# A two-layer hybrid decoder trunk on one core: the first projection chunk taken from raw token blocks, layer 0's norm applied afterwards

## The chip, the core and the metric

The kernel runs on one core of one Trainium2 chip. The core has a matrix engine (TensorE, in the profile PE for its matmuls and PEld for its weight loads), a vector engine (VectorE, DVE), a scalar engine (ScalarE, ACT), a general engine (GpSimd, POOL) and a queue engine (SyncE, SP) that issues nearly all DMAs here. SBUF is the working memory with 128 partitions; PSUM takes the matmul results, in banks of 128 x 512 float32. The engines run their own instruction streams in order and wait for each other by semaphores. The metric is the device time of one launch in microseconds (us); lower is better.

## The reference

The input `x` is 512 tokens of 2048 features, all in float32. Two layers follow, each as `x = x + rms_norm(mixer(rms_norm(x, norm_pre)), norm_post)`.

```python
def rms_norm(x, w):
    y = x * rsqrt(mean(x * x, axis=-1) + EPS)
    return y * w
# layer 0 (even): z = h @ w_in, 2048 -> 7 * 1024, split into qa, fa, ia, ga, ub, vb, gb
#   8 recurrence heads from qa, fa, ia (chunked gated linear recurrence, then rms_norm) * silu(ga)
#   8 gating groups: layer_norm(vb) per 128 columns, causal 128 x 128 mixing, + bias, * ub * silu(gb)
#   concatenation @ w_out
# layer 1 (odd): multi-head latent attention with rotary keys, silu gate, @ w_out
```

What matters for the change: `h` is `x` scaled per token by one factor r (the reciprocal root mean square) and per feature by `norm_pre`. Every column of `z` is linear in `h`, so r can be applied to `z` instead of to `x`. For `vb`, which goes through a layer norm, r cancels but for the epsilon.

## The kernel before

**Precision.** Matmuls use operands that are rounded to the faster `float32r` form. To keep float32 accuracy each operand is split into a rounded part (`hi`, written by ScalarE as a cast) and the rest (`lo`, written by VectorE as a subtraction), and three matmuls take the place of one: hi x hi, hi x lo, lo x hi. `R` holds the split activations, transposed: `R[:, 2k]` and `R[:, 2k+1]` are hi and lo of features 128k to 128k+127 for all 512 tokens.

**Weights.** `plan_chunk` lists the weight pieces, each of 128 x 1024 elements (512 KB), in the order of use. `fetch(n)` issues the DMA of a piece into one of three `raw` buffers, `wload` splits it into `whi` and `wlo` (four buffers each), and `piece(n)` sees that pieces up to n + 3 are split. `proj_tok` computes a chunk with tokens on the partitions of the result (the activations are the stationary operand); `proj_feat` computes one with features on the partitions. `tick()` is called after each piece and runs the small tasks that `at(delay, ...)` has put off, so that the recurrence work lies between the matmuls.

**Order.** The code is traced as a list, and a planner then makes one fixed instruction stream for each engine out of it. It works by dependencies and its own cost estimates, with trace order as the priority, so an instruction whose inputs and buffers are free may be placed well ahead of its place in the code.

**The start.** The norm weights of layer 0 come by DMA into four partitions of `B`, and VectorE spreads them over all (line 352). For each of the four token tiles, `pre_norm` squares the four 512-feature blocks on ScalarE (line 290), sums them, makes r on GpSimd (lines 275, 276), multiplies x by r and the weights on VectorE (line 296), transposes on TensorE, four 128 x 128 transposes to a PSUM bank `tp` of which there are two (line 301), and splits the result into `R` (lines 283, 284). The first chunk, `ia` for two heads, is 256 columns wide; its first four pieces are taken token tile by token tile (`by="first"`), so that it can start when the first tile is normalized. The `ia` columns of all eight heads come as 256 (heads 0 and 1), 512 (heads 2 to 5) and 256 (heads 6 and 7).

**The later chunks of layer 0.** For each of four pairs of heads p, `fa`, `qa` and `ga` follow; their evacuations (`fa_evac` and so on) write PSUM to `W`, which held x until then. `hgrn_vec`, `hgrn_scores`, `hgrn_state`, `hgrn_out` and `hgrn_fin` are the recurrence. Then come two `gmlp` halves, the output projection, and layer 1. These take PSUM from four `mm` banks in turn.

Of the kernel before, what the change touches and what calls it, by code (L numbers as in the profile page):

```python
# [10 lines left out]
F32 = mybir.dt.float32  # L11
# [7 lines left out]
P = 128  # L19
T = 512  # L20
NT = T // P
# [23 lines left out]
def trunk_kernel(ctx, tc, x, positions, norm_pre, norm_post, ev_w_in, ev_lb_logits, ev_a_onorm,  # L45
# [9 lines left out]
    ptp = ctx.enter_context(tc.tile_pool(name="ptp", bufs=2, space=bass.MemoryType.PSUM))  # L55

    def mm_bank():
        return pmm.tile([P, 512], F32, name="mm", tag="mm")
# [30 lines left out]

    def row_bc(dst, src_row):  # L90
        nc.sync.dma_start(out=dst, in_=src_row.partition_broadcast(P))


    W = new_w("Wa")
    for c in range(4):
        (nc.vector if c % 2 else nc.gpsimd).memset(B[:, 4 + c, :], 0.0)
    nc.sync.dma_start(out=B[0:P:32, 4:8, :],
                      in_=norm_pre[0].partition_broadcast(4).rearrange("q (c n) -> q c n", c=4))
    for c in range(4):
        nc.sync.dma_start(out=W[:, c, :], in_=x_t[0][:, c * 512:(c + 1) * 512])  # L100

# [4 lines left out]

    pk = const.tile([18, P], F32, name="pk")
    nc.sync.dma_start(out=pk[0:16, :], in_=ev_lb_logits.rearrange("l (h p) -> (l h) p", p=P))
    nc.sync.dma_start(out=pk[16:17, :], in_=ev_a_onorm)
    nc.sync.dma_start(out=pk[17:18, :], in_=inv_freq)  # L110

# [20 lines left out]
    def wview(w):  # L132
        return w.rearrange("(k p) c -> p k c", p=P)
# [13 lines left out]
    def fetch(n):  # L147
        src, nk, nco, _ = plan[n]
        raw = ring.tile([P, 1024], F32, name="raw", tag="raw", bufs=3)
        nc.sync.dma_start(out=raw[:, 0:nk * nco].rearrange("p (k c) -> p k c", k=nk), in_=src)  # L150
        fetched[n] = raw

    def wload(i):
# [12 lines left out]
        lo = ring.tile([P, 1024], F32R, name="wlo", tag="wlo")  # L166
        if cuts is None:
            nc.scalar.copy(hi[:, 0:n], raw[:, 0:n])  # L168
            nc.vector.tensor_tensor(lo[:, 0:n], raw[:, 0:n], hi[:, 0:n].bitcast(F32), ALU.subtract)  # L169
# [25 lines left out]
    def at(delay, fn):  # L195
        seq[0] += 1
        tasks.append((clock[0] + delay, seq[0], fn))
# [117 lines left out]


    ew, ow = wview(ev_w_in[0]), wview(od_w_in[0])
    qv, kvv = wview(od_w_qb[0]), wview(od_w_kvb[0])
    cuts_q = ((0, 128), (128, 192))
    pl = {}  # L320
    for p in range(4):
        if p == 1:
            pl["ia", p] = plan_chunk(ew, IA + 256, 512, KD, 2)
        elif p != 2:
            pl["ia", p] = plan_chunk(ew, IA + 256 * p, 256, KD, 4)
        for nm_, c0 in (("fa", FA), ("qa", QA), ("ga", GA)):
            pl[nm_, p] = plan_chunk(ew, c0 + 256 * p, 256, KD, 4)
# [21 lines left out]

    wpre = [B[:, 4 + c, :] for c in range(4)]  # L350
    for c in range(4):
        nc.vector.stream_shuffle(wpre[c], wpre[c], [0] * 32)
    for i in range(NT):
        if i > 0:
            for c in range(4):
                nc.sync.dma_start(out=W[:, 4 * i + c, :], in_=x_t[i][:, c * 512:(c + 1) * 512])
            if i == 1:
                issue_to(3)
        else:
            for q in range(2):  # L360
                fetch(q)
        pre_norm(i, [W[:, 4 * i + c, :] for c in range(4)], wpre,
                 [B[:, 8 + 4 * (i % 2) + c, :] for c in range(4)], G[:, 8, :])

# [4 lines left out]
    def setup_masks():  # L369
# [14 lines left out]
        nc.vector.memset(pw, 1.0)  # L384
        nc.gpsimd.memset(G[:, 8, :], 0.0)

    setup_masks()
    S_sb = new_hs("S_sb", F32)
    nc.gpsimd.memset(S_sb, 0.0)

# [3 lines left out]
    def setup_rope():  # L394
        pi = G[:, 6, :].bitcast(I32)
        row_bc(pi, positions[0])
        ang, n, r = sinT, cosT, G[:, 6, :]
# [154 lines left out]
    for p in range(4):  # L552
        def ia_evac(i, ps, p=p):
            psv = ps.rearrange("p (h v) -> p h v", v=P)
            for a in range(0, psv.shape[1], 2):
                vp = 2 * ((p + a // 2) % 2)
                nc.scalar.copy(G[:, vp:vp + 2, i * P:(i + 1) * P], psv[:, a:a + 2])
# [8 lines left out]
        def ga_evac(m, ps):  # L566
            nc.scalar.activation(W[:, 6 + m, :], ps, AF.Sigmoid)
            nc.vector.tensor_tensor(W[:, 6 + m, :], ps, W[:, 6 + m, :], ALU.mult)
# [12 lines left out]

    def gmlp(s_):
# [4 lines left out]
        wsT = G[:, 0, :]  # L587
        row_bc(lnw[0], ev_b_ln_w[0, s_ * 512:(s_ + 1) * 512])
        row_bc(lnw[1], ev_b_ln_b[0, s_ * 512:(s_ + 1) * 512])
        row_bc(bias, ev_b_bias[0, 4 * s_:4 * s_ + 4].rearrange("g t -> (g t)"))  # L590
        nc.sync.dma_start(out=ws, in_=ev_b_ws[0, 4 * s_:4 * s_ + 4].rearrange("g t s -> t g s"))
        nc.gpsimd.affine_select(ws, ws, pattern=[[0, 4], [-1, P]], compare_op=ALU.is_ge, fill=0.0,
# [13 lines left out]
        def vb_evac(i, ps):  # L606
            for g in range(4):
                nc.vector.bn_stats(stats[:, i, g], ps[:, g * P:(g + 1) * P])
                nc.vector.bn_aggr(mv[:, i, g], stats[:, i, g])
            nc.gpsimd.tensor_scalar(rs[:, i], mv[:, i, :, 1], 1.0, EPS, ALU.mult, ALU.add)  # L610
            nc.gpsimd.tensor_tensor(rs[:, i], rs[:, i], mhalf[:, 0:4], ALU.pow)
# [24 lines left out]
        for e in range(2):  # L636
# [3 lines left out]
            def ub_evac(m, ps, U=U):  # L640
                nc.scalar.copy(U[:, m], ps)

            def gb_evac(m, ps, p=p, Z=Z, V=V):
                nc.scalar.activation(Z[:, m], ps, AF.Sigmoid)
                nc.vector.tensor_tensor(Z[:, m], ps, Z[:, m], ALU.mult)
                nc.vector.tensor_tensor(B[:, 8 + 2 * p + m, :], V[:, m], Z[:, m], ALU.mult)
# [359 lines left out]
```

## Time and profile before

| | |
|---|---|
| time, median of three runs | 1597.62 us (1597.39 to 1598.52) |
| time of the profiled execution | 1596.93 us |
| its span | 1595.2 us |
| TensorE busy, share of the span | 1568.3 us, 98% |
| VectorE busy | 750.8 us, 47% |
| ScalarE busy | 532.0 us, 33% |
| GpSimd busy | 95.7 us, 6% |
| DMA, mean over the span | 101 GB/s |

A row of the timeline gives the start from the beginning of the span, the duration, the engine, the line of the kernel, the operation, its output and inputs, a count where equal instructions are merged, and in brackets the idle time before it with what ended it. A row of the groups gives the count after the shapes, then the busy time in us and the mean duration of one in ns. A row of the stretches gives for each engine the busy time and, after x, the count of its instructions. A row of the waits gives the total, the number of waits and the longest. Matmuls overlap in the trace: the duration of one is longer than the distance to the next, and the distance is what a stream of them costs.

### The profile page before, as it was taken

How to read it: one execution, taken by the hardware profiler on the slowest of the kernel's cores; microseconds unless marked ns; L12 is line 12 of the kernel's file. 1: busy time of each engine (PE TensorE's matmuls, PEld its weight loads, DVE VectorE, ACT ScalarE, POOL GpSimd, SP SyncE). 2: the span in 40 equal slices, each digit the busy share in tenths (PEclk: the TensorE clock that was granted, in tenths of full speed). 3: DMA queues.
4: the chain of work that ended last, by engine and by line, in shares of the span. 5: the costliest groups of instructions: out<-in, count | busy, mean ns of one | idle time of the engine just before them, and what ended most of it. 6: DMA issues, size and time to landing. Idle time of an engine off the chain costs nothing. (4 is left out here: it accounts for less than half of the span.)

```text
span 1595.2 us, 19593 instructions
## 1 busy us (share of the span) xinstructions
PE 1568.3 (98%) x7841; PEld 1327.2 (83%) x7841; DVE 750.8 (47%) x1333; ACT 532.0 (33%) x904; POOL 95.7 (6%) x145
## 2 busy tenths in 40 slices
PE   6999999999999999999999999999999999999997
PEld 6888888898888888888887788888889988988886
DVE  7653455535434224353225743232266767762234
ACT  6422322222222222232224533222265555542221
POOL 1000000000014004000001000000000000000000
PEclk9999999999999999999999999999999999999999
DMA  7332222223234333243335523333221221332324
GB/s 221 118 92 80 92 93 80 80 80 99 91 102 119 99 98 101 94 151 100 102 103 172 150 78 102 93 93 98 87 75 55 70 60 52 102 106 94 105 93 158
DMA packets 118150, 160.95 MB, mean 101 GB/s; under 512 B 7830, under 2 KB 74408, under 8 KB 118056
## 3 DMA queue, kind: packets, MB, share of 16 engines
q1 hardware_dynamic: 118060, 159.71, 32.4%
q8 instruction: 61, 1.00, 0.3%
q14 instruction: 29, 0.24, 0.0%
HBM read 151.30 MB, written 8.39 MB: 100 GB/s over the span
## 5 line engine op out<-in xcount | busy, mean ns | idle before, releaser
L169 DVE TENSOR_TENSOR wlo<-raw,whi 128x1024 fp32r<-128x1024 f32 x240 | 296.8, 1238 | 641.3 <-ACT whi L168 624.8
L168 ACT CAST whi<-raw 128x1024 fp32r<-128x1024 f32 x240 | 252.3, 1052 | 779.1 <-PE mm L211 346.3
L209 PE MATMUL mm<-whi,R 128*128 128x512 f32 (+1 forms) x960 | 364.0, 379 | 0.5 <-ACT R L283 0.5
L210 PE MATMUL mm<-wlo,R 128*128 128x512 f32 (+1 forms) x960 | 362.1, 377 | 1.2 <-DVE wlo L169 1.2
L211 PE MATMUL mm<-whi,R 128*128 128x512 f32 (+1 forms) x960 | 362.1, 377 | 0.0
L214 PE MATMUL mm<-R,whi 128*128 128x512 f32 x832 | 326.1, 392 | 0.0
L216 PE MATMUL mm<-R,wlo 128*128 128x512 f32 x832 | 324.0, 389 | 0.0
L215 PE MATMUL mm<-R,whi 128*128 128x512 f32 x832 | 323.9, 389 | 0.0
L210 PEld LDWEIGHTS mm<-wlo,R 128*128 128x128 f32 x960 | 181.6, 189 | 33.3 <-DVE wlo L169 2.0
L209 PEld LDWEIGHTS mm<-whi,R 128*128 128x128 f32 x960 | 181.6, 189 | 33.0 <-ACT R L283 1.2
L211 PEld LDWEIGHTS mm<-whi,R 128*128 128x128 f32 x960 | 181.5, 189 | 32.5
L216 PEld LDWEIGHTS mm<-R,wlo 128*128 128x128 f32 x832 | 156.1, 188 | 32.6
L214 PEld LDWEIGHTS mm<-R,whi 128*128 128x128 f32 x832 | 156.2, 188 | 32.2
L215 PEld LDWEIGHTS mm<-R,whi 128*128 128x128 f32 x832 | 156.2, 188 | 32.0
L214 PE MATMUL mm<-Wc,whi 128*128 128x512 f32 x160 | 62.9, 393 | 0.0
L216 PE MATMUL mm<-Wc,wlo 128*128 128x512 f32 x160 | 62.6, 391 | 0.0
L215 PE MATMUL mm<-Wc,whi 128*128 128x512 f32 x160 | 62.4, 390 | 0.0
L284 DVE TENSOR_TENSOR R<-mm,R 128x512 fp32r<-128x512 f32 x48 | 32.9, 686 | 27.9 <-ACT R L283 27.9
L284 DVE TENSOR_TENSOR R<-tp,R 128x512 fp32r<-128x512 f32 x64 | 42.3, 684 | 4.2 <-ACT R L283 3.5
L283 ACT CAST R<-tp 128x512 fp32r<-128x512 f32 x64 | 35.9, 587 | 20.4 <-PE tp L301 18.2
L896 ACT ACTIVATE G<-sc,nm 128x512 f32<-128x512 f32 (+2 forms) x48 | 26.1, 545 | 41.2 <-DVE nm L895 41.2
L283 ACT CAST R<-mm 128x512 fp32r<-128x512 f32 x48 | 28.2, 587 | 32.2 <-PE mm L211 18.3
(243 smaller groups left out, 1645.9 us busy)
## 6 DMA issues: line engine op xcount, KB each, us to landing
raw<-in_ev_w_in_dram SPq DMA_DIRECT2D x112, 512.0 KB, 3.6
raw<-in_od_w_in_dram SPq DMA_DIRECT2D x49, 512.0 KB, 3.8
raw<-in_ev_w_out_dram SPq DMA_DIRECT2D x32, 512.0 KB, 3.6
raw<-in_od_w_out_dram SPq DMA_DIRECT2D x32, 512.0 KB, 3.7
raw<-in_od_w_kvb_dram SPq DMA_DIRECT2D x16, 512.0 KB, 3.6
raw<-in_od_w_qb_dram SPq DMA_DIRECT2D x16, 384.0 KB, 3.2
Wa<-in_x_dram SPq DMA_DIRECT2D x16, 256.0 KB, 6.3
G<-in_x_dram SPq DMA_DIRECT2D x16, 256.0 KB, 4.2
```

Of the source, the lines that this page charges most:

```text
L168: nc.scalar.copy(hi[:, 0:n], raw[:, 0:n])
L169: nc.vector.tensor_tensor(lo[:, 0:n], raw[:, 0:n], hi[:, 0:n].bitcast(F32), ALU.subtract)
L209: nc.tensor.matmul(o, hh[:, sl], wh, start=first, stop=False, skip_group_check=True)
L210: nc.tensor.matmul(o, hh[:, sl], wl, start=False, stop=False, skip_group_check=True)
L211: nc.tensor.matmul(o, hl[:, sl], wh, start=False, stop=last, skip_group_check=True)
L214: nc.tensor.matmul(ps, hi, hh, start=first, stop=False)
L215: nc.tensor.matmul(ps, hi, hl, start=False, stop=False)
L216: nc.tensor.matmul(ps, lo, hh, start=False, stop=last)
L283: nc.scalar.copy(dst_hi, src)
L284: nc.vector.tensor_tensor(dst_lo, src, dst_hi.bitcast(F32), ALU.subtract)
L896: nc.scalar.activation(pv[j], sp[j], AF.Exp, bias=nm[:, j:j + 1], scale=C_SCALE, accum_out=su[:, j:j + 1])
```

## The change

`pre_norm` is no longer used for layer 0. The 512 tokens by 2048 features of x are loaded in 16 blocks of 128 tokens x 512 features, interleaved with the first three weight pieces. The transposes act on raw x. A pair of 128 x 128 blocks (`flip_x`) is split while it is multiplied by the norm weight, which is now one number per partition (`ncol`, itself transposed from a 16 x 128 load). Squares, sums and the factor r (`rn`) are made during the first chunk and applied behind the matmuls: `ia` by ScalarE's scale when it is evacuated, `fa`, `qa`, `ga`, `ub`, `gb` by a VectorE product with `rb` (r spread over the partitions by four matmuls, `spread_rn`), and `vb` through the epsilon of its layer norm (`eps_rn`).

The first chunk is now `ia` for four heads, 512 columns wide, worked off piece by piece with the four token tiles inside (`first_chunk`); the second `ia` chunk, also 512 wide, comes at p = 2. The instructions of TensorE, ScalarE and VectorE traced in the first chunk keep their traced order (`in_order`). Ahead of and behind the first flip stand 6 and 8 transposes of the identity (`idle_turns`) whose results are not used. The first weight piece is split in two halves. Several DMAs are held in their traced order on SP.

```diff
+    def load_x(i, c):
+        tc.keep_in_program_order(nc.sync.dma_start(out=W[:, 4 * i + c, :],
+                                                   in_=x_t[i][:, c * 512:(c + 1) * 512]))
+    load_x(0, 0)
...
-        if cuts is None:
-            nc.scalar.copy(hi[:, 0:n], raw[:, 0:n])
-            nc.vector.tensor_tensor(lo[:, 0:n], raw[:, 0:n], hi[:, 0:n].bitcast(F32), ALU.subtract)
+        if cuts is None or cuts == "halves":
+            step = n if cuts is None else n // 2
+            for a in range(0, n, step):
+                e = slice(a, a + step)
+                nc.scalar.copy(hi[:, e], raw[:, e])
+                nc.vector.tensor_tensor(lo[:, e], raw[:, e], hi[:, e].bitcast(F32), ALU.subtract)
...
+    def square(i, c):
+        nc.scalar.activation(G[:, 7, :], W[:, 4 * i + c, :], AF.Square, scale=D ** -0.5,
+                             accum_out=pss[:, i, c:c + 1])
+    def factor():
+        nc.vector.tensor_reduce(rms[:, 2], pss, AX.X, ALU.add)
+        nc.gpsimd.tensor_scalar(rms[:, 2], rms[:, 2], EPS, None, ALU.add)
+        nc.gpsimd.tensor_tensor(rn, rms[:, 2], mhalf[:, 0:4], ALU.pow)
+        nc.gpsimd.tensor_scalar(eps_rn, rms[:, 2], EPS, None, ALU.mult)
+    def spread_rn():
+        tp = tp_bank()
+        for i in range(NT):
+            nc.tensor.matmul(tp[:, i * P:(i + 1) * P], rn[:, i:i + 1].broadcast_to([P, P]), ident,
+                             start=True, stop=True)
+        nc.scalar.copy(rb, tp)
+    def flip_x(n):
+        q, i = n // NT, n % NT
+        if q > 7:
+            return
+        tp = tp_bank()
+        sl = slice(i * P, (i + 1) * P)
+        for j in range(2):
+            o = (2 * q + j) % 4 * P
+            nc.tensor.transpose(tp[:, j * P:(j + 1) * P], W[:, 4 * i + q // 2, o:o + P], ident)
+        parts = [(2 * q + j, ncol[:, 2 * q + j:2 * q + j + 1], tp[:, j * P:(j + 1) * P]) for j in range(2)]
+        for k, w, src in parts:
+            nc.scalar.activation(R[:, 2 * k, sl], src, AF.Copy, scale=w)
+        for k, w, src in parts:
+            nc.vector.scalar_tensor_tensor(R[:, 2 * k + 1, sl], src, w, R[:, 2 * k, sl].bitcast(F32),
+                                           ALU.mult, ALU.subtract)
+    def first_chunk(first, evac):
...
+        idle_turns(6)
+        flip_x(0)
+        idle_turns(8)
+        issue_to(first)
+        flips = iter(range(1, 8 * NT + 4))
+        for q in range(8):
+            if q + 3 < 8:
+                fetch(first + q + 3)
+            if q < 2:
+                for t in range(NT):
+                    load_x(t, 2 + q)
+            for i in range(NT):
+                if q > 0 or i > 1:
+                    flip_x(next(flips))
+                mms(q, i, 0)
+                if q == 0 and i < 2:
+                    flip_x(next(flips))
+                mms(q, i, 1)
+                if q == 0 and i < 2:
+                    flip_x(next(flips))
+                if i == (0 if q else 1) and q < 7:
+                    issue_to(first + q + 1)
+                if q in (1, 3, 4, 6):
+                    square(i, {1: 0, 3: 1, 4: 2, 6: 3}[q])
+                if q == 7:
+                    evac(i, outs[i])
+            ready.pop(first + q)
+            if q == 6:
+                factor()
+            tick()
...
+    fetch(0)
+    for i in range(1, NT):
+        load_x(i, 0)
+    fetch(1)
     for i in range(NT):
...
+        load_x(i, 1)
+        if i == 1:
+            fetch(2)
...
         def fa_evac(m, ps):
+            nc.vector.tensor_tensor(ps, ps, rb, ALU.mult)
             nc.scalar.activation(W[:, m, :], ps, AF.Sigmoid)
...
         def qa_evac(m, ps):
-            nc.scalar.copy(W[:, 4 + m, :], ps)
+            nc.vector.tensor_tensor(W[:, 4 + m, :], ps, rb, ALU.mult)
...
         if p == 0:
-            at(1, setup_cols)
-            at(12, setup_rope)
-        if p != 2:
-            proj_tok(pl["ia", p], 512 if p == 1 else 256, r_act, KD, ia_evac, by="first" if p == 0 else "piece")
+            at(2, setup_masks)
+            at(7, load_pk)
+            at(9, spread_rn)
+            at(11, setup_cols)
+            at(16, setup_rope)
+            with in_order():
+                first_chunk(pl["ia", p], ia_evac)
+        elif p == 2:
+            proj_tok(pl["ia", p], 512, r_act, KD, ia_evac)
```

`ga_evac`, `gb_evac` and `ub_evac` change like `fa_evac` and `qa_evac`; the loads of `positions` and of the `gmlp` parameters are held in traced order too.

More of the change, by code (lines that the diff above doesn't have):

```diff
@@ L1 @@
-from contextlib import ExitStack
+from contextlib import ExitStack, contextmanager
 import numpy as np
@@ L55, in trunk_kernel, with in_order @@
     ptp = ctx.enter_context(tc.tile_pool(name="ptp", bufs=2, space=bass.MemoryType.PSUM))
+    @contextmanager
+    def in_order():
+        traced = nc.cur_bb.bb.instructions
+        start, prev = len(traced), {}
+        yield
+        for ins in traced[start:]:
+            if ins.engine in (mybir.EngineType.PE, mybir.EngineType.Activation, mybir.EngineType.DVE):
+                if ins.engine in prev:
+                    tc.add_manual_dep(ins, prev[ins.engine],
+                                      mybir.DependencyInfo(mybir.DependencyClass.NoSync,
+                                                           mybir.DependencyReason.DATA), reason="in_order")
+                prev[ins.engine] = ins.name
     def mm_bank():
@@ L88, in trunk_kernel, with row_bc @@
     x1_t = x1_dram.rearrange("(i p) d -> i p d", p=P)
-    def row_bc(dst, src_row):
-        nc.sync.dma_start(out=dst, in_=src_row.partition_broadcast(P))
+    def row_bc(dst, src_row, held=False):
+        ins = nc.sync.dma_start(out=dst, in_=src_row.partition_broadcast(P))
+        if held:
+            tc.keep_in_program_order(ins)
     W = new_w("Wa")
[L95 to L100, printed above, removed]
+    nrow = B[0:16, 0, 0:P]
+    nc.sync.dma_start(out=nrow, in_=norm_pre[0].rearrange("(k p) -> k p", p=P))
+    def load_x(i, c):
+        tc.keep_in_program_order(nc.sync.dma_start(out=W[:, 4 * i + c, :],
+                                                   in_=x_t[i][:, c * 512:(c + 1) * 512]))
+    load_x(0, 0)
     ident = const.tile([P, P], F32, name="ident")
@@ L105, in trunk_kernel, with load_pk @@
     nc.gpsimd.memset(mhalf, -0.5)
[L107 to L110, printed above, removed]
+    ncol = const.tile([P, KD], F32, name="ncol")
+    pk = B[0:18, 1, 0:P]
+    def load_pk():
+        tc.keep_in_program_order(
+            nc.sync.dma_start(out=pk[0:16, :], in_=ev_lb_logits.rearrange("l (h p) -> (l h) p", p=P)))
+        tc.keep_in_program_order(nc.sync.dma_start(out=pk[16:17, :], in_=ev_a_onorm))
+        tc.keep_in_program_order(nc.sync.dma_start(out=pk[17:18, :], in_=inv_freq))
     cols = const.tile([P, 18], F32, name="cols")
@@ L149, in fetch @@
         raw = ring.tile([P, 1024], F32, name="raw", tag="raw", bufs=3)
-        nc.sync.dma_start(out=raw[:, 0:nk * nco].rearrange("p (k c) -> p k c", k=nk), in_=src)
+        ins = nc.sync.dma_start(out=raw[:, 0:nk * nco].rearrange("p (k c) -> p k c", k=nk), in_=src)
+        if n < 8:
+            tc.keep_in_program_order(ins)
         fetched[n] = raw
@@ new lines, in first_chunk, with mms, idle_turns @@
+    def first_chunk(first, evac):
+        outs = [mm_bank() for _ in range(NT)]
+        def mms(q, i, kk):
+            k = 2 * q + kk
+            wh, wl = ready[first + q]
+            tok_steps(outs[i], r_act, k, slice(i * P, (i + 1) * P), wh[:, kk], wl[:, kk], k == 0, k == KD - 1)
+        ntp = sc_bank()
+        nc.tensor.transpose(ntp[:, 0:KD], nrow, ident[0:KD, 0:KD])
+        nc.vector.tensor_copy(ncol, ntp[:, 0:KD])
+        def idle_turns(n):
+            for _ in range(n):
+                nc.tensor.transpose(ntp[:, P:2 * P], ident, ident)
+        idle_turns(6)
[28 more added lines that the diff above has]
+            tick()
@@ L321, in trunk_kernel @@
     for p in range(4):
[L322 to L325, printed above, removed]
+        if p % 2 == 0:
+            pl["ia", p] = plan_chunk(ew, IA + 256 * p, 512, KD, 2, "halves" if p == 0 else None)
         for nm_, c0 in (("fa", FA), ("qa", QA), ("ga", GA)):
@@ L385, in setup_masks @@
         nc.gpsimd.memset(G[:, 8, :], 0.0)
-    setup_masks()
+        nc.gpsimd.memset(S_sb, 0.0)
     S_sb = new_hs("S_sb", F32)
-    nc.gpsimd.memset(S_sb, 0.0)
     cosT = const.tile([P, T], F32, name="cosT")
@@ L395, in setup_rope @@
         pi = G[:, 6, :].bitcast(I32)
-        row_bc(pi, positions[0])
+        row_bc(pi, positions[0], True)
         ang, n, r = sinT, cosT, G[:, 6, :]
```

35 lines of the change are left out of this document (15 added, 20 removed).

## The prediction

> **What bounds the kernel now.** I read the page's totals first, then the work by stretches, what TensorE waited for, and last the timeline of the start.
>
> ```profile
> span 1595.2 us, 19593 instructions
> PE 1568.3 (98%) x7841; PEld 1327.2 (83%) x7841; DVE 750.8 (47%) x1333; ACT 532.0 (33%) x904; POOL 95.7 (6%) x145
> ```
> ```profile
> 0.00:40.00 40.00, 26.72 (x183) 24.81 (x184) 30.21 (x62) 25.73 (x56) 6.95 (x24) 1.00 0.72 221
> 40.00:200.00 160.00, 160.00 (x806) 135.27 (x806) 77.41 (x113) 47.84 (x69) 7.62 (x16) 1.00 0.31 95
> ```
> ```profile
> PE tp L301 <- DVE B L296: 15.2, 8, 10.7
> PE mm L210 <- DVE wlo L169: 1.2, 2, 0.8
> ```
>
> TensorE sets the time. From 40 us it is busy without a gap; before, it is busy for 26.7 of 40 us, and nearly all its waits are those of the transposes for normalized x. So the change can give what the first 40 us waste, and whatever it does to the count of TensorE's cycles. The start:
>
> ```profile
> 0.79 0.87 SPq L100 DMA_DIRECT2D Wa<-in_x_dram  x2
> ...
> 2.14 0.29 POOL masks.py:199 TENSOR_SCALAR_AFFINE_SELECT ident<-ident 128x128 f32<-128x128 f32 x1
> ...
> 3.95 0.63 ACT L290 ACTIVATE G<-Wa 128x512 f32<-128x512 f32 x1 [1.88 <-DMA Wa<-in_x_dram]
> ...
> 4.48 0.19 ACT L290 ACTIVATION_READ_ACCUMULATOR G<-Wa 128x1 f32 x1
> ...
> 4.79 0.94 SPq L150 DMA_DIRECT2D raw<-in_ev_w_in_dram  x2
> 5.00 0.63 ACT L290 ACTIVATE G<-Wa 128x512 f32<-128x512 f32 x1 [0.33 <-DMA Wa<-in_x_dram]
> ...
> 9.30 1.04 ACT L168 CAST whi<-raw 128x1024 fp32r<-128x1024 f32 x1 [1.58 <-DMA raw<-in_ev_w_in_dram]
> ...
> 10.69 1.97 PE L301 MATMUL tp<-ident,B 128*128 128x128 f32 x8 [10.69 <-DVE B L296]
> ...
> 12.48 0.58 PE L209 MATMUL mm<-whi,R 128*128 128x256 f32 x1
> ...
> 14.42 1.11 PE L301 MATMUL tp<-ident,B 128*128 128x128 f32 x4
> ...
> 19.38 0.41 PE L211 MATMUL mm<-whi,R 128*128 128x256 f32 x1
> ...
> 19.60 0.37 PE L209 MATMUL mm<-whi,R 128*128 128x256 f32 x1
> ...
> 19.80 0.28 PE L210 MATMUL mm<-wlo,R 128*128 128x256 f32 x1
> ...
> 19.92 0.28 PE L211 MATMUL mm<-whi,R 128*128 128x256 f32 x1
> ```
>
> Three losses: no TensorE work up to 10.69, a broken start to 14.42, and matmuls at half rate to about 19.7 (0.22 us from one 256-wide matmul to the next at 19.38, 0.12 at 19.80). The granted clock is shown as 1.00 throughout, so it has no record there; the distances show the step. It came 9.0 us after the first transpose and 5.3 us after the stream had become dense.
>
> What a stream costs at full rate, from the timelines at 30 and 42 us and near the end:
>
> ```profile
> 30.26 0.28 PE L211 MATMUL mm<-whi,R 128*128 128x256 f32 x1
> 30.38 0.60 PE L301 MATMUL tp<-ident,B 128*128 128x128 f32 x4
> 30.73 0.37 PE L209 MATMUL mm<-whi,R 128*128 128x256 f32 x1
> 30.94 0.28 PE L210 MATMUL mm<-wlo,R 128*128 128x256 f32 x1
> ...
> 42.08 0.28 PE L209 MATMUL mm<-whi,R 128*128 128x256 f32 x1
> ...
> 44.96 0.28 PE L209 MATMUL mm<-whi,R 128*128 128x256 f32 x1
> ```
> ```profile
> 1583.85 0.39 PE L209 MATMUL mm<-whi,R 128*128 128x512 f32 x1
> ...
> 1585.66 0.39 PE L211 MATMUL mm<-whi,R 128*128 128x512 f32 x1
> ```
>
> A 256-wide matmul takes 2.88 / 24 = 0.120 us, a 512-wide one 1.81 / 8 = 0.226 us, and four transposes among matmuls 0.35 + (0.21 - 0.12) = 0.44 us. Of the 183 instructions up to 40 us, 64 are transposes (row below) and one is that of the constants (line 118):
>
> ```profile
> 0.00:40.00 40.00, 11.45 (x64) 8.35 (x64) 1.00 0.72 221
> ```
>
> That is 118 x 0.120 + 16 x 0.44 + 0.1 = 21.3 us of work in 40 us: **18.7 us are lost**, the most that an earlier and denser start could return.
>
> **The change, part by part.** Durations for the new small operations:
>
> ```profile
> L168 ACT CAST whi<-raw 128x1024 fp32r<-128x1024 f32 x240 | 252.3, 1052 | 779.1 <-PE mm L211 346.3 <-PE mm L215 327.9 <-issue 61.8
> L290 ACT ACTIVATE G<-Wa 128x512 f32<-128x512 f32 x32 | 20.2, 632 | 10.0 <-DVE Wa L684 6.7 <-DMA Wa<-in_x_dram 2.7
> L515 ACT COPY G<-sc 128x128 f32<-128x128 f32 x8 | 2.1, 258 | 0.0
> ```
> ```profile
> L169 DVE TENSOR_TENSOR wlo<-raw,whi 128x1024 fp32r<-128x1024 f32 x240 | 296.8, 1238 | 641.3 <-ACT whi L168 624.8 <-PE sc L628 11.9 <-PE tp L735 4.2
> L568 DVE TENSOR_TENSOR Wa<-mm,Wa 128x512 f32<-128x512 f32 x8 | 5.5, 684 | 2.8 <-ACT Wa L567 2.8
> L517 DVE SCALAR_TENSOR_TENSOR G<-G,btot,sc 128x128 f32<-128x128 f32 x16 | 5.4, 338 | 0.7 <-ACT G L515 0.6
> ```
>
> *First matmul.* SP's order becomes norm row, x block, first weight piece, three x blocks, second piece and so on, 0.44 us per issue. The first x block took 3.95 - 0.79 = 3.15 us; issued at 1.23 it lands near 4.4. The piece is issued at 1.66. Before, the first one took 9.30 - 4.79 = 4.5 us, with x ahead of it, which gives 6.2; 256 KB more took 5.00 - 3.95 = 1.05 us, so 512 KB behind the block gives 6.5. I take 6.2, with 5.3 and 7.5 as ends. Half a cast, between 0.53 and 1.05, say 0.6, gives 6.8. On TensorE stand the norm row's transpose, 6 identity ones, a flip, 8 more, each 0.22 us while the clock is low (eight between 10.69 and 12.48). They start when the norm row has landed, at 3.95 if it takes as long as the x block, at 2.9 if its few bytes save the 1.05 us of 256 KB (`ident` is ready at 2.4), and 17 x 0.22 = 3.7 us later they end, at 6.6 to 7.7. First matmul **7.2**; the second waits 0.3 for its lo half.
>
> *Later transfers.* Ahead of the chunk stand eight x blocks and three pieces, 3.5 MB, at 256 KB per 1.05 us some 15 us, so the last of them lands near 18; its flip comes with the third piece, after 20. The fetch of the fourth piece waits on SP until the first is split (about 8.3) and holds back x blocks that are needed at the fifth piece, after 30. No cost.
>
> *The clock.* Dense from 7.5, the rate steps up 5.3 us later, at 12.8, if only a matmul stream opens it, losing half, 2.7 us; if the identity transposes count from about 3.5, at 8.8, losing 0.7; by the 9.0 us from the first operation, at 12.5, losing 2.5. I take **2.0**, ends 0.7 and 3.4.
> [...] The trace cannot decide: its first transposes were followed by gaps.
>
> *Inside the chunk.* One of 32 steps is six 512-wide matmuls and a pair of transposes: 6 x 0.226 + 0.27 = 1.63 us (a pair is half of 0.35 plus the same 0.09). ScalarE per step: two of 0.26, a quarter of a cast, and in half of the steps a square of 0.63 with its 0.19 read-out, at most 1.6 us. VectorE: two of 0.34 and a quarter of 1.24, 1.0 us. A flip is three steps ahead of its matmuls, so this hides; where it does not, 16 steps with squares would expose a few tenths each. The masks, now traced behind the second piece, put a memset and four selects on GpSimd (five of at most 0.29 by the row at 2.14) ahead of VectorE's next flip halves, whose bank is wanted two steps (3.3 us) later. For waits for x blocks, masks and ScalarE together I take **1.0** us, ends 0 and 4.
>
> Lost at the start: 7.2 + 0.3 + 2.0 + 1.0 = 10.5 us against 18.7: **gain 8.2**.
>
> *TensorE's count.* 384 matmuls of 256 columns become 192 of 512: 384 x 0.120 - 192 x 0.226 = 46.1 - 43.4, **gain 2.7**. Transposes in 32 pairs for 16 fours: 32 x 0.27 - 16 x 0.44 = **1.6 lost**, ends 0 and 1.6. Four matmuls that spread r, priced as four transposes: **0.5 lost**.
>
> *What moves to VectorE.* Each feature projection gets two products of 0.68 us, 1.4 us in 22 us. The fullest stretch had
>
> ```profile
> 360.00:382.00 22.00, 22.00 (x101) 18.17 (x100) 14.38 (x23) 6.20 (x8) 3.10 (x5) 1.00 0.34 105
> ```
>
> so 15.8 of 22. The banks freed later are wanted a projection later, or 2.7 us later where a 512-wide chunk follows. Nothing on TensorE; without that cover it is 1.4 us per projection. The normalization taken away lay after 11 us beside matmuls. The held parameter loads are needed 17 us or more after their issue.
>
> Sum against the profiled run's 1596.93 us: 8.2 + 2.7 - 1.6 - 0.5 = 8.8, so 1588.1. The median of the runs shown is 0.7 above it: **1588.8 us**.
>
> **The rivals.**
>
> *The clock opens late*: only the matmul stream opens it, and the identity transposes merely fill TensorE's queue. The loss is 2.7 to 3.4, say 3.1, in place of 2.0, and the first matmul stands behind them at 7.6: 1588.8 + 1.1 + 0.4 = 1590.3. For it: the step came only after a dense stretch. Against it: there was no stretch of transposes alone to judge by. [...]
>
> *The chunk's end.* The first chunk splits one piece ahead only, so `fa` begins with its first piece unsplit unless the planner places fetch and split early. If it does not, TensorE waits for a landing, a cast and a subtraction:
>
> ```profile
> raw<-in_ev_w_in_dram SPq DMA_DIRECT2D x112, 512.0 KB, 3.6
> ```
>
> 3.6 + 1.05 + 1.24 = 5.9 us: 1594.7, no measurable change. Against it: the planner does place early; the load of the `gmlp` norm weights, traced hundreds of us later, was issued at
>
> ```profile
> 35.35 0.34 SPq L91 DMA_DIRECT2D B<-in_ev_b_ln_w_dram  x1
> ```
>
> *The flip's loop becomes the bound* (slower). A bank's turn is transposes 0.27, their end 0.25 later (0.60 against 0.35 above), ScalarE 0.52 and VectorE 0.68: 1.7 us, so two banks allow a step of 0.9. If a cast (1.05), a square (0.82) and a subtraction (1.24) all stand in the way, a turn is 4.8 and a step 2.4 against 1.63. In the 16 steps with squares that costs 16 x 0.8 = 12.8 us: 1601.6. It decides once a turn exceeds 3.26 us, that is, if the fixed order puts more than one of these ahead of every flip. Against it: a cast comes once in four steps.
>
> *VectorE late for the recurrence.* Eight heads at 1.4 us each for products ahead of their chain: 11 us, so 1600, no measurable change. Against it: TensorE waited for none of it before.
>
> **How the numbers follow.** Forecast 0.52, late clock 0.31, chunk's end 0.07, flip loop 0.06, VectorE 0.04. A measurement of this kernel can tell about 0.2%, 3.2 us, from no change, so faster means below 1594.4: 0.52 + 0.31 = 0.83; same 0.07 + 0.04 = 0.11; slower 0.06. The range: all good ends (first matmul 6.7, clock 0.7, no waits, no cost of pairs) give 4.5 us below the forecast, 1584.3; the bad ends of the costs (first matmul 7.7, clock 3.4 and 1.0 more of waits) give 1588.8 + 0.5 + 1.4 + 1.0 = 1591.7, and the chunk's end 1594.7. I take 1584.5 to 1594.5.
>
> **What would show it.** First matmul of the chunk near 7.2, distances of 0.226 from about 12 at the latest; 24 matmuls and 8 transposes per piece in 6.5 us; `fa` starting at about 62; no wait of TensorE for the products of `flip_x`, or for VectorE in the recurrence. Wrong, if TensorE idles between the first chunk and `fa`, or if flips wait for banks throughout.

## The result and the profile after

The changed kernel takes **1587.29 us** (median of four executions, 1586.94 to 1588.10); the kernel before took 1597.51 us beside it (1596.74 to 1598.52). The ratio is **0.9936, 95% interval 0.9922 to 0.9951**: 10.2 us or 0.64% faster. The forecast was 1588.8 us, in a range of 1584.5 to 1594.5. The profiled execution of the changed kernel took 1588.1 us, the longest of the four.

The totals of the profile after (busy time of each engine, its share of the span, the count of instructions):

```profile
span 1586.1 us, 19329 instructions
PE 1567.9 (99%) x7672; PEld 1317.3 (83%) x7672; DVE 769.4 (49%) x1401; ACT 536.1 (34%) x946; POOL 95.5 (6%) x138
```

Its work by stretches (TensorE matmuls, weight loads, VectorE, ScalarE, GpSimd, each with its count, then granted clock, DMA share, GB/s):

```profile
0.00:40.00 40.00, 35.99 (x169) 28.72 (x170) 20.92 (x67) 26.18 (x76) 3.14 (x14) 1.00 0.61 211
```

And what TensorE waited for:

```profile
PE tp L330 <- DVE B L325: 3.2, 4, 1.6
PE sc L394 <- DMA B<-in_norm_pre_dram: 2.5, 1, 2.5
PE tp L377 <- DMA Wa<-in_x_dram: 0.8, 1, 0.8
...
PE tp L377 <- DVE R L382: 0.4, 1, 0.4
```

TensorE is busy for 36.0 of the first 40 us where it was for 26.7. The 15.2 us of waits for normalized x have shrunk to 3.2, and those that are left belong to layer 1's norm, which the change does not touch. In their place stand small waits ahead of the first matmul: for the norm row, and for the first block of x. VectorE has 18.6 us more to do. At the start TensorE waits for it 0.3 us for the column of norm weights, 0.3 us for the lo half of the first weights and 0.4 us for a half of one flip; no wait for the new products shows.

The start, from TensorE's timeline of the kernel after:

```profile
2.50 0.25 PE L394 MATMUL sc<-ident,B 16*128 16x16 f32 x1 [2.50 <-DMA B<-in_norm_pre_dram]
3.02 1.54 PE L399 MATMUL sc<-ident 128*128 128x128 f32 x6 [0.27 <-DVE ncol L395]
5.36 0.69 PE L377 MATMUL tp<-ident,Wa 128*128 128x128 f32 x2 [0.79 <-DMA Wa<-in_x_dram]
5.84 1.91 PE L399 MATMUL sc<-ident 128*128 128x128 f32 x8
7.47 0.79 PE L238 MATMUL mm<-whi,R 128*128 128x512 f32 x1
8.20 0.80 PE L239 MATMUL mm<-wlo,R 128*128 128x512 f32 x1
...
10.07 0.63 PE L239 MATMUL mm<-wlo,R 128*128 128x512 f32 x1
10.50 0.63 PE L240 MATMUL mm<-whi,R 128*128 128x512 f32 x1
...
11.88 0.38 PE L377 MATMUL tp<-ident,Wa 128*128 128x128 f32 x2
12.02 0.48 PE L238 MATMUL mm<-whi,R 128*128 128x512 f32 x1
12.34 0.39 PE L239 MATMUL mm<-wlo,R 128*128 128x512 f32 x1
12.56 0.40 PE L240 MATMUL mm<-whi,R 128*128 128x512 f32 x1
...
13.63 0.44 PE L377 MATMUL tp<-ident,Wa 128*128 128x128 f32 x2 [0.44 <-DVE R L382]
```

The first matmul of the chunk starts at 7.47 instead of 12.48 us. The distances show the clock: 0.43 us from one 512-wide matmul to the next while the clock is low (from 10.07 to 10.50), 0.22 from 12.34 to 12.56. The trace also keeps a record of the granted clock, whose first stretch at full rate begins at 11.02 us, and at 19.77 in the kernel before. (The views give 1.00 ahead of it too, where nothing is recorded.) The end of the chunk:

```profile
24.92 0.38 PE L377 MATMUL tp<-ident,Wa 128*128 128x128 f32 x2
...
34.55 0.38 PE L377 MATMUL tp<-ident,Wa 128*128 128x128 f32 x2
...
60.86 0.39 PE L240 MATMUL mm<-whi,R 128*128 128x512 f32 x1
61.09 0.39 PE L243 MATMUL mm<-R,whi 128*128 128x512 f32 x1
```

`fa` (line 243) follows at 61.09 without a gap. From the pair of transposes at 24.92 to the one at 34.55 it is six steps, so a step of six matmuls and a pair takes 1.605 us. Counted back from the last matmul, each matmul after about 450 us starts 9.3 to 9.5 us earlier than its counterpart before. So the whole gain arises in layer 0, and nothing behind it takes any back. The last matmul starts at 1576.16 instead of 1585.66, 9.5 us earlier; the tail behind it is 0.4 us longer, so the span is 9.1 us shorter.

### The profile page after: what moved, and what is told of

The parts are those of the page before. It is cut to its first block, busy times and chain, and to the rows that moved or that the text cites. A ratio compares the mean times of both kernels' runs of the same rounds, so it can differ in the third digit from the quotient of the medians.

```text
span 1586.1 us, 19329 instructions
## 1 busy us (share of the span) xinstructions
PE 1567.9 (99%) x7672; PEld 1317.3 (83%) x7672; DVE 769.4 (49%) x1401; ACT 536.1 (34%) x946; POOL 95.5 (6%) x138
## 5 line engine op out<-in xcount | busy, mean ns | idle before, releaser
L198 DVE TENSOR_TENSOR wlo<-raw,whi 128x1024 fp32r<-128x1024 f32 (+1 forms) x248 | 297.5, 1203 | 594.7 <-ACT whi L197 574.2
L197 ACT CAST whi<-raw 128x1024 fp32r<-128x1024 f32 (+1 forms) x248 | 253.2, 1025 | 766.1 <-PE mm L240 323.9
L238 PE MATMUL mm<-whi,R 128*128 128x512 f32 x896 | 354.5, 396 | 0.6 <-ACT R L312 0.6
L240 PE MATMUL mm<-whi,R 128*128 128x512 f32 x896 | 350.3, 391 | 0.0
L239 PE MATMUL mm<-wlo,R 128*128 128x512 f32 x896 | 350.0, 391 | 0.0
L240 PEld LDWEIGHTS mm<-whi,R 128*128 128x128 f32 x896 | 168.5, 188 | 35.1
L238 PEld LDWEIGHTS mm<-whi,R 128*128 128x128 f32 x896 | 168.6, 188 | 34.3 <-ACT R L312 1.1
L239 PEld LDWEIGHTS mm<-wlo,R 128*128 128x128 f32 x896 | 168.7, 188 | 33.5 <-DVE wlo L198 0.7
L238 PE MATMUL mm<-whi,Wc 128*128 128x256 f32 x128 | 36.7, 287 | 0.0
L240 PE MATMUL mm<-whi,Wc 128*128 128x256 f32 x128 | 36.2, 283 | 0.0
```

The costliest lines, as they stand in the source:

```text
L197: nc.scalar.copy(hi[:, e], raw[:, e])
L198: nc.vector.tensor_tensor(lo[:, e], raw[:, e], hi[:, e].bitcast(F32), ALU.subtract)
L238: nc.tensor.matmul(o, hh[:, sl], wh, start=first, stop=False, skip_group_check=True)
L239: nc.tensor.matmul(o, hh[:, sl], wl, start=False, stop=False, skip_group_check=True)
L240: nc.tensor.matmul(o, hl[:, sl], wh, start=False, stop=last, skip_group_check=True)
```

## The experiments

Each kernel ran beside the kernel before (1597.24 to 1597.45 us in these runs). Times are medians of 5 to 11 executions, and ratios are against the kernel before. Unless the text says otherwise an edit starts from the changed kernel. The two theories on the clock: **A**, the identity transposes count as activity and open it; **B**, only matmuls open it, and the transposes are filling.

**The changed kernel again** (`a_again`), as the base of the others.

> The changed kernel once more, beside the experiments. Expected 1587.3 us, within 0.5; TensorE's first matmul of the chunk at 7.5 us and the step to full rate near 11 us, as in its first profile.

1586.74 us (1586.35 to 1587.49), ratio 0.9934 [0.9922, 0.9947]. The clock's record has the step at 9.18 us, where the first profile had 11.02, and `fa` starts at 60.34 instead of 61.09. The time is 0.6 us below the expected one, and the step is not near 11 us. Half of the 1.84 us by which the step is earlier is 0.9; the first matmul starts 0.14 later (7.61 for 7.47), which leaves 0.8, and matmul by matmul, 0.75 us separate the two executions at 12 us and 0.78 at 800 us. So the moment of the step differs from one execution to the next, and half of that difference is lost or won.

**No identity transposes** (`e1_no_turns`).

```diff
-        idle_turns(6)
         flip_x(0)
-        idle_turns(8)
```

> The 14 identity transposes are left out. Theory A (they count as activity and open the clock early): the matmuls still begin near 7.5 us, since the first weight piece lands at 6.8, but the full rate comes only 5 us after a dense stream, at 12.5 to 14, and the kernel is 0.8 to 1.5 us slower than the changed kernel. Theory B (only matmuls count): the full rate comes at the same place, near 11 us, and the time is the same or up to 0.3 us less.

1588.34 us (1588.16 to 1588.90), ratio 0.9945 [0.9933, 0.9958]: 1.6 us more than with them. TensorE's timeline:

```profile
7.63 0.80 PE L238 MATMUL mm<-whi,R 128*128 128x512 f32 x1 [1.49 <-ACT whi L197]
...
12.36 0.63 PE L240 MATMUL mm<-whi,R 128*128 128x512 f32 x1
...
13.46 0.39 PE L239 MATMUL mm<-wlo,R 128*128 128x512 f32 x1
```

The first matmul starts at 7.63, as with the transposes (7.61), so they delay nothing. The half rate lasts to 13.21 us by the clock's record, and `fa` starts at 62.24, 1.9 us later. In the eight profiled executions that have the 14 transposes and the held order (two of the changed kernel, and `e3_two_256`, `e4_narrow`, `e6_alt_halves`, `e7_two_products`, `e9_alt_four_banks`, `e10_free_loads` below) the step comes between 8.27 and 11.02 us, so 13.21 lies outside their spread. This agrees with A; the loss is a little more than A's 0.8 to 1.5 us.

**Identity matmuls in place of transposes** (`e2_mm_turns`).

```diff
-                nc.tensor.transpose(ntp[:, P:2 * P], ident, ident)
+                nc.tensor.matmul(ntp[:, P:2 * P], ident, ident, start=True, stop=True)
```

> The 14 identity transposes become 14 plain matmuls of the identity with itself, of the same size. Theory A (transposes count as much as matmuls): the same as the changed kernel, full rate near 11 us. Theory B (only matmuls count): the full rate comes up to 3.4 us earlier, near 7.6 to 9 us, and the kernel is 1 to 1.7 us faster than the changed kernel.

1586.85 us (1586.18 to 1587.34), ratio 0.9935 [0.9922, 0.9949]: no difference from transposes. The rows:

```profile
3.07 2.93 PE L399 MATMUL sc<-ident 128*128 128x128 f32 x12 [0.27 <-DVE ncol L395]
...
6.22 1.97 PE L399 MATMUL sc<-ident 128*128 128x128 f32 x16
7.95 0.47 PE L238 MATMUL mm<-whi,R 128*128 128x512 f32 x1
```

A plain float32 matmul leaves two records, and six of them take 2.93 us where six transposes took 1.54. The clock opens at 6.25 us, but the first matmul stands behind them at 7.95. Both effects nearly cancel: `fa` starts at 59.98 for 60.34. Since kind and amount changed together, this run does not separate A from B.

**A stretch of transposes alone, in the kernel before** (`e11_before_turns`): 48 identity transposes as soon as `ident` is made. Before, `PE` had nothing to do until 10.69 us.

```diff
+    turns = sc_bank()
+    for _ in range(48):
+        nc.tensor.transpose(turns[:, 0:P], ident, ident)
```

> The kernel before, with 48 identity transposes ahead of its first transpose of x, where TensorE was idle, and nothing else changed. If transposes open the clock: full rate before the first matmul at 12.5 us instead of at 19.8, so the dense part from 14.4 saves up to half of 5.3 us: 1.5 to 2.7 us faster than the kernel before, unless VectorE's normalization holds it back. If they do not count: the same time as before, full rate near 19.8.

1599.57 us (1598.25 to 1601.38), ratio 1.0015 [1.0006, 1.0024]: **slower** by 2.2 us, which neither theory had foreseen. On the clock the trace is clear. First the stretches for line 106 (the 48 transposes) alone, then for all instructions:

```profile
3.00:6.00 3.00, 3.00 (x16) 3.00 (x15) 1.00 0.81 247
7.00:9.50 2.50, 2.50 (x25) 2.50 (x24) 1.00 0.94 317
```
```profile
13.00:23.00 10.00, 5.51 (x24) 5.22 (x25) 8.05 (x11) 7.10 (x16) 0.75 (x2) 0.52 0.93 266
```

Sixteen transposes in 3.0 us, then 25 in 2.5: their distance falls from 0.213 to 0.109 us at the 20th, at 6.6 us, when TensorE has done nothing but transposes. **A is shown: transposes open the clock**, here 4.1 us after the first of them at 2.49. Then it closes again: the record has half rate from 13.42 to 23.66 us (0.52 in the mean between 13 and 23 us). The 48 transposes end before 10 us, and TensorE's rows show what came next; ScalarE's, first of the kernel before, then of this one, show what it waited for:

```profile
11.10 1.32 PE L304 MATMUL tp<-ident,B 128*128 128x128 f32 x8 [1.16 <-DVE B L299]
16.18 0.58 PE L212 MATMUL mm<-whi,R 128*128 128x256 f32 x1 [3.76 <-ACT R L286]
```
```profile
11.84 0.59 ACT L283 CAST R<-tp 128x512 fp32r<-128x512 f32 x1 [1.50 <-PE tp L301]
```
```profile
12.67 0.63 ACT L293 ACTIVATE G<-Wa 128x512 f32<-128x512 f32 x1
...
15.47 0.19 ACT L293 ACTIVATION_READ_ACCUMULATOR G<-Wa 128x1 f32 x1
15.56 1.05 ACT L286 CAST R<-tp 128x512 fp32r<-128x512 f32 x2
```

The flip's cast on ScalarE, at 11.84 us in the kernel before, now stands behind all four squares of the second token tile and starts at 15.56. The first matmul comes 3.7 us later (16.18 for 12.48), after a gap of 3.8 us. From the end of the 48 at 9.93 us to the closing at 13.42, TensorE worked for 1.3 us, on eight transposes. At 42 us the kernel is still 1.84 us behind the one before. That the planner took TensorE for occupied and so moved the cast back is inferred from the order; it was not tried, and neither was why the clock closed. So this kernel shows how the clock opens, but not what the transposes would be worth in the kernel before with its order kept.

**The second `ia` chunk in two of 256 columns** (`e3_two_256`).

```diff
+        elif p > 1:
+            pl["ia", p] = plan_chunk(ew, IA + 256 * p, 256, KD, 4)
...
-        elif p == 2:
-            proj_tok(pl["ia", p], 512, r_act, KD, ia_evac)
+        elif p > 1:
+            proj_tok(pl["ia", p], 256, r_act, KD, ia_evac)
```

> The second ia chunk (512 wide at p = 2) becomes two chunks of 256 columns, at p = 2 and p = 3. By the count of TensorE (0.120 us per 256-wide matmul, 0.226 per 512-wide): 384 x 0.120 - 192 x 0.226 = 2.7 us slower than the changed kernel. By the rival that the width does not matter and all of the gain is the start: no difference.

1590.02 us (1588.88 to 1590.69), ratio 0.9953 [0.9941, 0.9966]: 3.3 us more than the changed kernel. The start is untouched (`fa` at 60.28, the clock at 9.19). This is the term for TensorE's count, 2.7 us by the forecast. In the profiles the price is smaller: from the start of `fa` to the last matmul it is 1517.58 us here and 1515.07 and 1515.23 in the two profiles of the changed kernel, 2.4 us.

**The first chunk 256 wide** (`e4_narrow`): raw x, flips and clock as changed, but `ia` as 256, 512, 256 columns.

```diff
-            wh, wl = ready[first + q]
+            wh, wl = ready[first + q // 2]
...
-        if p % 2 == 0:
-            pl["ia", p] = plan_chunk(ew, IA + 256 * p, 512, KD, 2, "halves" if p == 0 else None)
+        if p == 1:
+            pl["ia", p] = plan_chunk(ew, IA + 256, 512, KD, 2)
+        elif p != 2:
+            pl["ia", p] = plan_chunk(ew, IA + 256 * p, 256, KD, 4, "halves" if p == 0 else None)
```

> The start of the changed kernel with a first chunk of 256 columns (ia then comes as 256, 512, 256 as before). By TensorE's count alone: 2.7 us slower than the changed kernel. By ScalarE's load, 32 pairs of scaled halves at 0.62, four casts at 1.05, 16 squares at 0.75, 36 us in all against 192 x 0.12 + 32 x 0.235 = 30.6 us of TensorE, the chunk would be bound by ScalarE: 5 to 6 us more than that, 8 us slower in all, so that about 2 us of the whole gain are left.

1595.53 us (1594.75 to 1596.37), ratio 0.9990 [0.9981, 0.9999]: nearly the whole gain is gone, 8.8 us more than the changed kernel where 8 were expected. The count of matmuls is 2.4 to 3.3 us of it (`e3_two_256`). As to the rest, TensorE waited for

```profile
PE tp L377 <- DVE R L382: 4.1, 6, 1.3
```

which is 0.4 us in the changed kernel: with 256 columns the matmuls of a step take half as long (0.120 us each for 0.226 by the rows of the kernel before), while the flip's work on ScalarE and VectorE stays the same (0.62 and 0.61 us a pair in the changed kernel). The width of the chunk is what hides the flips. The edit also puts four results into two PSUM banks and moves their evacuation behind the chunk; these were not tried alone.

**Without the held order of instructions** (`e5_free_order`).

```diff
-            with in_order():
-                first_chunk(pl["ia", p], ia_evac)
+            first_chunk(pl["ia", p], ia_evac)
```

> The order pins of the first chunk are taken away; the planner places its instructions. If the fixed order does no harm and gives nothing (what the prediction's sum supposes, which has no term for it): within 1 us of the changed kernel. If the order is part of the gain: the planner runs flips and squares by its own estimates, TensorE waits for halves, and it is 2 to 6 us slower.

1592.02 us (1590.78 to 1593.99), ratio 0.9967 [0.9956, 0.9979]: 5.3 us more. VectorE's and ScalarE's timelines:

```profile
7.47 1.29 DVE L198 TENSOR_TENSOR wlo<-raw,whi 128x512 fp32r<-128x512 f32 x2 [5.69 <-ACT whi L197]
8.68 0.17 DVE L395 COPY ncol<-sc 128x16 f32<-128x16 f32 x1
```
```profile
11.63 0.63 ACT L353 ACTIVATE G<-Wa 128x512 f32<-128x512 f32 x1 [0.23 <-DVE mask L487]
...
12.26 0.61 ACT L380 ACTIVATE R<-tp,ncol 128x128 fp32r<-128x128 f32 x2
```

The small copy of the norm weights, which every flip needs, stands behind the first split; the first flip stands behind squares and a wait for the mask. The first matmul starts at 12.66, where it started before the change.

**The halves of a pair alternating** (`e6_alt_halves`): ScalarE's half, VectorE's half, then the second pair of halves, instead of both ScalarE halves first.

```diff
         for k, w, src in parts:
             nc.scalar.activation(R[:, 2 * k, sl], src, AF.Copy, scale=w)
-        for k, w, src in parts:
             nc.vector.scalar_tensor_tensor(R[:, 2 * k + 1, sl], src, w, R[:, 2 * k, sl].bitcast(F32),
                                            ALU.mult, ALU.subtract)
```

> ScalarE and VectorE halves of a pair are traced alternately instead of both ScalarE halves first. Each engine's own order is the same. By the theory that a flip hides behind three steps: within 0.5 us of the changed kernel. By the rival that the loop of the two transpose banks is near its limit: VectorE's first half starts 0.3 us earlier or later, the waits of 0.4 us in the first piece change, and the time by 0.5 to 1.5 us.

1594.98 us (1594.14 to 1595.69), ratio 0.9984 [0.9975, 0.9993]: **8.2 us more**, which neither expectation had. Neither ScalarE's nor VectorE's own order changes. What ScalarE waited for ahead of its flip halves, in all (first 66 us), and one pair on the timeline:

```profile
  DVE R L381: 15.3, 29
```
```profile
36.27 0.35 ACT L380 ACTIVATE R<-tp,ncol 128x128 fp32r<-128x128 f32 x1
...
36.65 0.35 DVE L381 SCALAR_TENSOR_TENSOR R<-tp,ncol,R 128x128 fp32r<-128x128 f32 x1
37.04 0.37 ACT L380 ACTIVATE R<-tp,ncol 128x128 fp32r<-128x128 f32 x1 [0.42 <-DVE R L381]
37.42 0.63 ACT L353 ACTIVATE G<-Wa 128x512 f32<-128x512 f32 x1
37.44 0.35 DVE L381 SCALAR_TENSOR_TENSOR R<-tp,ncol,R 128x128 fp32r<-128x128 f32 x1 [0.44 <-ACT R L380]
```

In the changed kernel ScalarE's flips wait for TensorE alone (14.3 us, 19 times, time in which it has nothing to do), but for one wait for the norm weights at the start. Here its second half waits for VectorE's first: both halves of a pair lie in one PSUM bank, and the program orders their readers as traced. Rows of the changed kernel bear this out:

```profile
32.32 0.62 ACT L380 ACTIVATE R<-tp,ncol 128x128 fp32r<-128x128 f32 x2
...
33.44 0.63 ACT L380 ACTIVATE R<-tp,ncol 128x128 fp32r<-128x128 f32 x2
```
```profile
32.98 0.61 DVE L382 SCALAR_TENSOR_TENSOR R<-tp,ncol,R 128x128 fp32r<-128x128 f32 x2 [0.35 <-ACT R L380]
```

VectorE's first half needs only ScalarE's first, yet it starts behind both (32.32 + 0.62 = 32.94). That the bank orders them, and not the tile `R` which both write, shows in the next flip: it lies in the other bank, and ScalarE starts on it at 33.44, while VectorE still writes `R` until 33.59. With the halves alternating, a pair holds ScalarE from 36.27 to 37.42, 1.15 us, where two halves in a row take 0.62. With a square (0.63 and 0.19 for its read-out) a step no longer fits in 1.61 us, and `fa` starts at 68.59.

**The same, with four banks for the flips** (`e9_alt_four_banks`): alternating halves, and every second flip in a bank of the `sc` kind.

```diff
-        tp = tp_bank()
+        tp = sc_bank() if n % 2 else tp_bank()
```

> The halves traced alternately as in the kernel that took 1595.0, but with four PSUM banks for the flips (two of them taken from the sc banks, idle here). If the two banks set the loop there: most of the 8 us come back, 1587 to 1589. If ScalarE is the bound, because its second half now waits for VectorE's first (0.37 + 0.42 + 0.37 + a square's 0.8 is 2.0 us per step against 1.61 of TensorE, in half of the steps): still 1593 to 1595.

1592.82 us (1591.99 to 1593.70), ratio 0.9973 [0.9963, 0.9984]. Of the 8.2 us, 2.2 come back. So a lack of banks is the smaller part of that loss, and the time is just below the range that was expected with ScalarE as the bound. The profile agrees: from 13 to 60 us ScalarE is busy for 34.1 us and waits 12.9 us for VectorE's halves, 47.0 us of 47, so it has no slack left.

**A second product behind each projection** (`e7_two_products`): each evacuation of `fa`, `qa`, `ga`, `ub`, `gb` multiplies once more on VectorE, by one.

```diff
+            nc.vector.tensor_tensor(ps, ps, one.broadcast_to([P, 512]), ALU.mult)
```

> Each fa, qa, ga, ub and gb evacuation gets a second VectorE product (by a constant one), 40 more of 0.68 us, 27 us of VectorE work. By the prediction's step that these products cost TensorE nothing: within 0.5 us of the changed kernel. By the rival that they delay the recurrence's chain: 1.4 us per head or 11 us slower.

1587.51 us (1586.65 to 1588.21), ratio 0.9937 [0.9923, 0.9950]: 0.8 us more than the base by the medians, for some 27 us of added VectorE work (40 products; those of the changed kernel take 0.68 to 0.70 us). That is a little more than the 0.5 expected and far from the rival's 11. From the start of `fa`, behind which all these products lie, to the last matmul the profile has 1515.37 us, 0.1 to 0.3 us more than the changed kernel's two. The products of the change are hidden.

**First loads in halves** (`e8_halved_loads`): plain identity matmuls, 6 and 4 of them, and the first block of x and the first weight piece each loaded by two DMAs. It was meant as a better version.

```diff
-    load_x(0, 0)
+    load_x(0, 0, 0, 256)
...
+        step = nk // 2 if n == 0 else nk
+        for a in range(0, nk, step):
+            ins = nc.sync.dma_start(out=raw[:, a * nco:(a + step) * nco].rearrange("p (k c) -> p k c", k=step),
+                                    in_=src[:, a:a + step])
...
-                nc.tensor.transpose(ntp[:, P:2 * P], ident, ident)
+                nc.tensor.matmul(ntp[:, P:2 * P], ident, ident, start=True, stop=True)
...
-        idle_turns(8)
+        idle_turns(4)
...
+    load_x(0, 0, 256, 512)
```

> The turns become plain matmuls, 6 and 4 instead of 6 and 8 transposes; the first x block and the first weight piece are each loaded in two halves, so that a flip and the first matmuls need half the bytes. If the start is bound by the landing of the first piece (6.8 us) and the clock: the first matmul comes 0.5 to 1 us earlier, at full rate, and the kernel is 1 to 1.8 us faster than the changed kernel. If other waits take the place (x blocks of the other tiles, flips): no difference beyond 0.5.

1586.93 us (1586.38 to 1587.57), ratio 0.9936 [0.9923, 0.9948]: the same as the changed kernel. The clock opens at 6.48, but the first matmul stays at 7.65. The edit's two parts work against each other:

```profile
5.80 0.63 PE L380 MATMUL tp<-ident,Wa 128*128 128x128 f32 x2
```

The first flip starts here without a wait, right behind the six plain matmuls, where it starts at 5.36 in the changed kernel; its halves on ScalarE, and the cast of the first weights behind them (at 6.98 for 6.80), come later too. So the run does not show what earlier loads alone would bring.

**Without the held order of the loads** (`e10_free_loads`): all seven lines that hold a DMA, of which one is shown.

```diff
+    free = lambda ins: ins
...
-            tc.keep_in_program_order(ins)
+            free(ins)
```

> The loads are no longer held in their traced order on SP. By the prediction's step that this order costs and gives nothing: within 0.5 us of the changed kernel. By the rival that the order matters: x blocks and parameter loads are then issued ahead of weight pieces, TensorE waits for a piece inside the first chunk, 1 to 4 us slower.

1588.67 us (1587.41 to 1589.63), ratio 0.9946 [0.9934, 0.9959]: 1.9 us more, as by the rival, but not for a weight piece. What TensorE, and one row of VectorE, waited for:

```profile
PE tp L378 <- DVE R L383: 2.5, 2, 2.0
```
```profile
24.94 0.43 DVE L507 CAST sinT<-G 128x512 f32<-128x512 int32 x1 [4.27 <-DMA G<-in_positions_dram]
```

A cast for layer 1's rotary tables was placed on VectorE inside the chunk and waits 4.3 us for its positions; two flips of x are queued behind it, and TensorE waits for them. `fa` starts at 62.21, 1.9 us later than in the changed kernel.

## Why the prediction was right

**The bound.** The prediction took the first 40 us as the place of the gain. Matmul by matmul the whole gain lies in layer 0, as said above.

**The sum.** For the profiled execution it gave 1588.1 us, and that execution took 1588.1. That they agree to the tenth is luck: the execution was the longest of four, and some terms were off and cancel:

| step of the prediction | forecast | in the profile after |
|---|---|---|
| first matmul of the chunk | 7.2 us | 7.47 us |
| second matmul's wait | 0.3 us | 0.3 us: 8.20 - 7.47 - 0.43 |
| clock's half rate | 2.0 us lost | 1.8 us: (11.02 - 7.47) / 2 |
| waits inside the chunk | 1.0 us | 0.4 us, the wait at 13.63 |
| all lost at the start | 10.5 us | 9.7 us: 61.09 - 32 x 1.605 (the rows above give 10.0; one pair, 0.25, lies ahead of the first matmul) |
| TensorE's count | 2.7 us gained | 2.4 us by the profiles of `e3_two_256`, 3.3 by its medians |
| transposes in pairs | 1.6 us lost | 0.9 us: 32 x 0.249 - 16 x 0.44 |
| matmuls that spread r | 0.5 us lost | 0.9 us |

By the right column the gain is 18.7 - 9.7 + 2.4 - 0.9 - 0.9 = 9.6 us, and the last matmul did start 9.5 us earlier; by the left one it is 8.8. Of those 9.5 us the longer tail and 0.3 us outside the span took 0.7, for which the forecast had no term. (The good ends of the prediction's range, 0.5, 1.3, 1.0 and 1.6, add up to 4.4 us, not 4.5.)

*The pairs* were 0.7 us too dear. The prediction charged each pair the full disturbance of the next matmul that four transposes had shown, 0.09 us, on half of their own 0.35. The rows from 11.88 on give 0.14 for the pair and 0.32 - 0.226 = 0.09 for the matmul behind it: the pair itself was the part that was too dear. A whole step leaves 1.605 - 6 x 0.226 = 0.249 us for the pair, instead of 0.27, since the later matmuls of a step lose a little too.

*The spreading matmuls* were priced as transposes, and a plain float32 matmul takes twice as long (2.93 us for six where six transposes took 1.54, in `e2_mm_turns`):

```profile
66.53 1.05 PE L365 MATMUL tp<-ident,rms 128*128 128x128 f32 x8
```

Four are eight records, about 0.9 us.

*Loads.* The first block of x was issued when the forecast had it:

```profile
1.24 0.41 SPq L115 DMA_DIRECT2D Wa<-in_x_dram  x1
```

It ended TensorE's wait at 5.36, 4.1 us later, where 3.15 had been taken from the kernel before. Why it took longer was not tried. The eight transposes behind its flip end with the first matmul's start at 7.47, inside the foreseen 6.6 to 7.7.

**The clock.** The prediction could not decide between two theories and took 2.0 us between 0.7 and 3.4. No profile of the new start shows the 3.4, or the 3.1 that a late opening was priced at: without any identity transposes (`e1_no_turns`) the half rate lasts from the first matmul at 7.63 to 13.21 us, which loses 2.8. In `e11_before_turns` the 20th transpose of a stretch of transposes alone runs at full rate (0.109 us apart from there, 0.213 before), so the rival "the clock opens late" falls. The clock's records have stretches of 6.83 us at full rate and 10.24 us at half rate (`e11_before_turns`), of 3.41 us at half rate (`e8_halved_loads`, below) and of 1570.13 us at full rate (both profiles of the changed kernel). The first two are twice and three times as long as the third. What sets these lengths was not shown, and neither was the cause of the spread between two executions of the changed kernel (9.18 and 11.02 us), for which the prediction's single value had no term.

**No wait at the chunk's end.** A piece takes 4 x 1.605 = 6.42 us where 6.5 were forecast, and `fa` follows at 61.09 against "about 62", without a gap: the rival with an unsplit first piece did not happen.

**The slower rival, the flips' loop,** did not happen, but there was little room. It was argued against by the casts' rarity alone, and ScalarE's half was priced at 0.26 us where two take 0.62: a step with a square asks 0.62 for the halves, 0.26 for a quarter of a cast and 0.82 for the square, 1.7 us of ScalarE in 1.605, and only the steps without squares make up for it. `e6_alt_halves` reaches a like loss by another way and one line: ScalarE's pair takes 1.15 us instead of 0.62, flips come late, and 8.2 us are lost where the rival had 12.8. The prediction added up ScalarE's and VectorE's times for a turn, but it did not see that the reads of one bank follow each other in traced order, and so it had no price for the order of the halves.

**Products on VectorE.** TensorE waits for none of them, as forecast, and twice as many cost 0.8 us by the medians.

**The held loads** were forecast to cost nothing. That was right, but the step was incomplete: holding them gains 1.9 us, and holding the instructions 5.3. The forecast priced the start as traced, and that holds only because the order is held.

Left open: what the identity transposes would bring in the kernel before with its order kept, what earlier first loads would bring, and what the splitting of the first weight piece in halves is worth, which no run varied.

## What to carry to other kernels

Where one engine is the bound, list what it loses at the start (late first operation, low clock, gaps) and what each step needs of the others, and check that the step of the bound is longer than each: here 512 columns hide what 256 do not. Trace order was a cost here where two engines read one PSUM bank: letting the engine with more to do read everything first was worth 8.2 us. Fill the idle start with transposes only if the order of the real work stays, and read the clock from the distances of equal instructions.

## What was not expected of the hardware

In `e8_halved_loads` the clock dropped for 3.41 us in the middle of the kernel. At the boundary of the layers TensorE waits briefly for layer 1's norm (3.2 us in four waits in the changed kernel, 2.7 us in two in `e8_halved_loads`); in two kernels (`e8_halved_loads`, `e10_free_loads`) the granted clock fell there, to 0.83 in the mean between 850 and 860 us, in the others it did not. Over the whole span of the profiled executions the mean clock is 0.997 in these two and 0.998 or 0.999 in the others, but for the 0.994 of `e11_before_turns`, whose drop stands above. The stretch in `e8_halved_loads`, then in the changed kernel:

```profile
850.00:860.00 10.00, 8.60 (x37) 6.88 (x38) 8.15 (x15) 5.11 (x15) 2.47 (x5) 0.83 0.88 256
```
```profile
850.00:860.00 10.00, 7.95 (x41) 5.86 (x40) 8.02 (x15) 6.09 (x17) 2.21 (x6) 1.00 0.87 268
```

By the clock's record it ran at half rate from 852.98 to 856.40 us, 3.41 us. The time from the start of `fa` to the last matmul is 1515.68 us there and 1515.07 to 1515.23 in the two profiles of the changed kernel, so the drop costs about 0.5 us; in `e10_free_loads` it is 1515.70. It takes back what `e8_halved_loads` had won at the start (`fa` at 60.02 instead of 60.34). Since one execution of each kernel was profiled (two of the changed kernel), how often this happens is not known.
